# 24 key columns for the edge units of a neighbourhood attention, stacked products for the meta tokens, and the merges' weights split in an earlier stage

## The chip, the cores and the metric

The kernel runs on one core of a Trainium2 chip. The metric is the device time of one execution in microseconds (us); lower is better. Times are given as the median of repeated executions. Beside them stands one profiled execution, from which all durations are read.

## What is computed

The reference is one encoder layer, in float32, over two sequences: a prompt of 1024 tokens and a sample of 2048 tokens, each with 16 learned meta tokens in front. Width is 1024. What matters here:

```
xn   = rmsnorm(h) ; proj = xn @ w_in + b_in          # 1024 -> 6672 columns
ya   = neighbourhood_attention(q, k, v, rpb) * silu(z) @ w_a
yb   = bidirectional_mlstm(...) * silu(z) @ w_b
y    = (sigmoid(ga) * ya + sigmoid(gb) * yb) @ w_out
out  = h + rmsnorm(y)                                # meta rows are dropped
```

The attention has 8 heads of 64. Tokens lie on a grid 64 wide. A query at column c sees 8 rows of keys and the 16 key columns from c0 = clip(c-8, 0, 48), plus the 16 meta tokens. Sixteen neighbouring query columns form a column block (four per grid row), and the reference takes 32 key columns for each block. For the first block (c from 0 to 15) c0 is 0 to 7, so its windows need key columns 0 to 22; for the last block c0 is 40 to 48, so they need columns 40 to 63. The two middle blocks need 31 columns each.

## The kernel before

**Precision.** Every float32 product is made of three products in a rounded format (`fp32r`): a value x is split into a high part xh (rounded by ScalarE with a copy) and a low part xl (x minus xh, by VectorE). Then `xh*wh + xh*wl + xl*wh` is summed in PSUM. `mm3` (L166 to L171) issues these three.

**Two streams of work, one order.** The program is written as two Python generators. `dense` (L1658) walks through `PLAN` (L41): groups of projection columns for a token range ("m" for the mLSTM's columns, "n" for the attention's, "g" for the merge gates), then six "f" entries, the final merges of 512 tokens each. `sparse` walks through `STEPS` (L42): mLSTM of the prompt, attention of the prompt, mLSTM of the sample (the long mLSTM), attention of the sample. Each generator yields costs in us that the author wrote in by hand; `run` (L1703) lets the dense stream advance until its costs have paid for the last sparse step. An attention unit yields four times `A_NA` = 1.085, so some 4.3 us of dense products lie between two units. The order of TensorE's instructions is the order in which these generators issue them. The order on the other engines and in the DMA queues is chosen by a scheduler that simulates the program.

**Weights.** The weights come in units of 128 partitions by up to 1056 values. `requests` (L661) writes the list of units in the order of use; "i" and "t" are the input projection's, "m" the merge's (w_a over w_b, 8 units) and "o" the output projection's (8 units). `wload` (L233) fetches at most two raw units ahead. `wpump` (L244) turns a unit into its two parts: the first time by a split (ScalarE at L263, VectorE at L264) after which both parts are also written to DRAM (`wflush`, L276), later by two loads of 512 KB each (L256). At most `NBW` = 4 units are out at a time (four buffers each for `whi` and `wlo`); `wtake` hands units to a job and `wdone` gives a buffer back. Before the change the "m" and "o" units are first met in the first final merge, and split there.

**Projection.** `fm_half` (L541) makes 128 output channels for 512 tokens with the weights as the stationary operand; `fm_evac` takes them out of PSUM. `tm_unit` (L570) makes 256 or 264 channels token by token with the tokens as the stationary operand (L590 to L592). In the first two groups it also does the 16 meta tokens: three products for each of 8 contraction steps with a stationary operand of only 16 columns.

**The first group.** The row scales of the prompt are not known when its products start. So `group` (L691) keeps the evacuations of the first columns back (`late`), gives them PSUM banks by a list of tags, and issues the product that spreads the row scales over the partitions (`rrows`, L317) inside a chosen column: column `lu` = 2 in the first half, `lu` = 3 in the second (L721).

**Attention.** A head works through four units, one for each column block (`cb`), over 8 query rows. `na_prep` (L817) loads and splits q, k and v for the next head in six steps spread over the units of the present one. It loads k twice, into partitions 0 to 63 and 64 to 127 (`twice`, L743), and rounds both at once into `kd` (L855); partitions 64 to 127 of the stationary operand hold the low part of q. For a unit `na_scores` (L867) issues two products over `ns` x 32 key columns (L877, L878; ns is 12, 13 or 16 rows, one of which holds the meta tokens), and VectorE adds the bias table (L881). `na_exp` takes the exponential, `na_scale` divides by the sum, `na_turn` transposes the probabilities in four blocks of 8 columns (L908) and rounds them (L910), `na_low` makes the low part (L915), and `na_out` multiplies by v, one product for each block (L923). There are 48 heads and 192 units; half of the units are edge units (`cb` 0 or 3).

**Merge.** `final` (L1496) makes `ya @ w_a` and `yb @ w_b` with `mm3`, gates and adds them, and multiplies by w_out (L1569 to L1571).

Of the kernel before, what the change touches and what calls it, by code (L numbers as in the profile page):

```python
# [17 lines left out]
P = 128  # L18
# [3 lines left out]
NM = 16  # L22
# [20 lines left out]
KC0 = (0, 8, 24, 32)  # L43
OFFC = (15, 7, 7, -1)
# [27 lines left out]
def _consts():  # L72
    onehot = np.zeros((64, 4, 8, 16), np.float32)
    for cb in range(4):
        for ic in range(16):
            c0 = min(max(cb * 16 + ic - 8, 0), 48)
            onehot[c0, cb, :, ic] = 1.0
    for ir in range(8):
        onehot[49 + ir, :, ir, :] = 1.0
    masks = np.zeros((3, 64, 16, 64), np.float32)  # L80
    R = 32
    for typ, tl in ((0, 0), (1, 1), (2, R // 8 - 1)):
        _, lo, n = _row_types(R)[tl]
        slots = list(range(lo, lo + n))
        slots = [None] + slots if typ == 2 else slots + [None]
        for si, row in enumerate(slots):
            for c0 in range(49):
                m = np.full(64, NEG, np.float32)
                if row is None:
                    m[(8 if c0 < 24 else 32):][:NM] = 0.0  # L90
# [30 lines left out]
class K:  # L121
# [122 lines left out]
    def wpump(self, most=NBW, parts=1, copy=None):  # L244


        nc, wp = self.nc, self.wp
        self.wload()
        while self.wraw and self.wout < most:
            key, raw, nk, w = self.wraw.popleft()  # L250
            n = nk * w
            hi = wp.tile([P, 4 * WU], F32R, name="whi", bufs=NBW)
            lo = wp.tile([P, 4 * WU], F32R, name="wlo", bufs=NBW)
            if raw is None:
                for x, d in zip((hi, lo), self.wkept[key]):
                    nc.sync.dma_start(x[:, :n].bitcast(F32), d[:, :])  # L256
            else:
                for a in range(parts):
                    c = slice(a * n // parts, (a + 1) * n // parts)
                    if copy:  # L260
                        copy(hi[:, c], raw[:, c])
                    else:
                        nc.scalar.activation(hi[:, c], raw[:, c], AF.Copy)  # L263
                    nc.vector.tensor_tensor(lo[:, c], raw[:, c], hi[:, c].bitcast(F32), op=ALU.subtract)  # L264
# [16 lines left out]
    def wtake(self, n):  # L281
        self.wpump()
        return [self.wrdy.popleft() for _ in range(n)]
# [69 lines left out]
    def opening(self, xp):  # L353
# [45 lines left out]
        self.wrp = wp, 2  # L399

# [93 lines left out]
    def fm_evac(self, col, s, t0, meta, chunks, ps):  # L494
# [39 lines left out]
        if meta and C_NK <= col < C_NV:  # L534
            km = wp.tile([P, 64], F32, name="km", bufs=1)
            nc.gpsimd.memset(km, 0.0)
            nc.gpsimd.tensor_copy(km[:, 8:24], st[:, :NM])
            nc.gpsimd.tensor_copy(km[:, 32:48], st[:, :NM])
            nc.sync.dma_start(self.NKM[(col % 512) // P][:, :], km)
# [30 lines left out]
    def tm_unit(self, col, halves, wd):  # L570
# [10 lines left out]
        for j, (x, s, c, n, cnt, tok) in enumerate(todo):  # L581
            st = wp.tile([P, 2, WU], F32, name="stT", bufs=4)
            for a in range(cnt):
                p = self.psum("pj", [P, 512])
                o = p[:n, :wd]
                xs = slice(c + a * P, c + a * P + n)
                for k in range(KT):
                    wh, wl = ws[k // 4][0][:, k % 4, :], ws[k // 4][1][:, k % 4, :]
                    xh, xl = x[0][:, k, xs], x[1][:, k, xs]
                    nc.tensor.matmul(o, xh, wh, start=k == 0, stop=False)  # L590
                    nc.tensor.matmul(o, xh, wl, start=False, stop=False)  # L591
                    nc.tensor.matmul(o, xl, wh, start=False, stop=k == KT - 1)  # L592
                    if k == 3:
                        if j == len(todo) - 1 and a == cnt - 1:
                            self.wdone()
                        yield 12 * C256
                if j == len(todo) - 1 and a == cnt - 1:
                    self.wdone()
                if s == 0:
                    r = 8 if tok is None else tok // P + a  # L600
# [5 lines left out]
                yield 12 * C256  # L606

    def tm_store(self, col, wd, s, n, cnt, tok, st):
# [30 lines left out]
        else:  # L639
            if tok is None:  # L640
                for lo in (8, 32):
                    nc.sync.dma_start(self.NVM[lo:lo + NM, f:f + wd], st[:n, 0, :wd])
# [18 lines left out]
    def requests(self):  # L661

        unit = {k: j for j, k in enumerate(_weight_units())}
        for s, t0, cols in PLAN:
            if s == "f":
                keys = [("m", f, P) for f in range(KT)] + [("o", c, a) for c in range(4) for a in range(2)]
# [24 lines left out]
    def group(self, s, t0, meta, cols, reuse, nxt):  # L691
# [4 lines left out]
        for j, (kind, c) in enumerate(jobs):  # L696
# [7 lines left out]
            for hf in range(2):  # L704
# [37 lines left out]

    def twice(self, out, d, r0, c0):  # L743

        for a in (0, 64):
            self.nc.sync.dma_start(out[a:a + 64], d[r0:r0 + 64, c0:c0 + out.shape[1]])
# [70 lines left out]
    def na_prep(self, np_, s, rows, heads, j):  # L817
# [14 lines left out]
        self.twice(kr[:, rs:rs + nr, :].rearrange("p a b -> p (a b)"), self.NK[s][pr], h0, lo * 64)  # L832
        self.twice(kr[:, ms, :], self.NKM[pr], h0, 0)
# [20 lines left out]
        with self.held():  # L854
            nc.scalar.activation(kd[:, :ns, :], kr[:, :ns, :], AF.Copy)  # L855
        yield
        nc.vector.tensor_tensor(kx[0:64, :ns, :], kr[0:64, :ns, :], kd[0:64, :ns, :].bitcast(F32), op=ALU.subtract)
# [9 lines left out]
    def na_scores(self, np_, unit, rows):  # L867
# [8 lines left out]
        so = sc[:, :N].rearrange("p (a b) -> p a b", b=32)  # L876
        nc.tensor.matmul(so, stk[:, cb, :], kd[:, :ns, kc:kc + 32], start=True, stop=False)  # L877
        nc.tensor.matmul(so, qb[:, cb, :], self.kx[hh][:, :ns, kc:kc + 32], start=False, stop=True)  # L878
# [3 lines left out]
            out=so, in0=so, in1=gt[:, g0:g0 + ns, c0:c0 + 32],  # L882
            op0=ALU.add, op1=ALU.min, scale=-1.0, scalar=3.0e38, accum_out=mx)
        unit[3] = (pr_, mx, N)
        unit[6] = sc

    def na_exp(self, np_, unit):
        nc = self.nc
        (pr_, mx, N), sc = unit[3], unit[6]
        sm = np_.tile([P, 1], F32, name="sm", bufs=4)  # L890
        nc.scalar.activation(pr_[:, :N].rearrange("p (b a c) -> p b a c", b=4, c=8),
                             sc[:, :N].rearrange("p (a b c) -> p b a c", b=4, c=8),
                             AF.Exp, bias=mx, scale=-1.0, accum_out=sm)
        unit[3] = (pr_, sm, N)

    def na_scale(self, np_, unit):
        nc = self.nc
        pr_, sm, N = unit[3]
# [3 lines left out]
    def na_turn(self, np_, unit):  # L902
        nc = self.nc
        pr_, _, N = unit[3]
        ks = N // 4
        pt = self.psum("tr", [P, 4, P])
        for ch in range(4):
            nc.tensor.transpose(pt[:ks, ch, :], pr_[:, ch * ks:(ch + 1) * ks], self.ident)  # L908
        pts = np_.tile([P, 4, 2, P], F32R, name="pts", bufs=2)
        nc.scalar.activation(pts[:ks, :, 0, :], pt[:ks], AF.Copy)  # L910
        unit[4], unit[6] = pts, pt

    def na_low(self, unit):
        pts, pt, ks = unit[4], unit[6], unit[3][2] // 4
        self.nc.vector.tensor_tensor(pts[:ks, :, 1, :], pt[:ks], pts[:ks, :, 0, :].bitcast(F32), op=ALU.subtract)  # L915

    def na_out(self, unit):
        nc = self.nc
        vt, cb, (_, _, N), pts = unit[0][3], unit[2], unit[3], unit[4]
        ks, kc = N // 4, KC0[cb]  # L920
        av = self.psum("sm", [P, 512])
        for ch in range(4):
            nc.tensor.matmul(av[:, :256], vt[:ks, kc // 8 + ch].rearrange("p a b -> p (a b)"),  # L923
                             pts[:ks, ch].rearrange("p a b -> p (a b)"), start=ch == 0, stop=ch == 3)
# [733 lines left out]
    def dense(self, ctx):  # L1658
# [3 lines left out]
        self.requests()  # L1662
        self.xp = ExitStack()
# [5 lines left out]
        for j, (s, t0, cols) in enumerate(PLAN):  # L1669
# [12 lines left out]
            if not self.done:  # L1682
                z = self.wp.tile([P, 64], F32, name="km", bufs=1)
                self.nc.gpsimd.memset(z, 0.0)
                for lo in (0, 24, 48, 56):
# [3 lines left out]
    def sparse(self):  # L1689

        for kind, s, rts in STEPS:
# [4 lines left out]
            else:  # L1696
                types = _row_types(SEQLEN[s] // 64)
# [81 lines left out]
```

## Time and profile before

| what | value |
|---|---|
| median of 3 executions | 2786.84 us (2786.1 to 2787.6) |
| the profiled execution's own time | 2792.15 us |
| its span, first to last instruction | 2790.4 us |
| mean granted TensorE clock | 0.997 |
| TensorE products | 17120 records |
| DMA | 655.09 MB, mean 235 GB/s |

Stages in the profiled execution, in us from the span's start: mLSTM of the prompt within 298 to 760, attention of the prompt 760 to 1130, long mLSTM 1176 to 1927, attention of the sample 1927 to about 2676. The final merges start at about 2091 and run to the end, the first one to 2215.

A "timeline" row gives the start, the duration, the engine, the source line, the operation, the tile written and the tiles read, and the shape. The duration of a product contains its way through the array, and products overlap; what one costs in a stream is the distance from its start to the next start. A "waits" row gives the total, the number and the longest of the waits of one line for another. A "windows" row gives, for a stretch, each engine's busy time with its instruction count, then the granted clock, the DMA share and GB/s. A "groups" row ends in: busy us, mean ns of one | idle time before them, and what ended it.

### The profile page before, as it was taken

Reading aid. Unit: us, or ns where it says so; the run is one execution under the profiler, and the core shown is the slowest. Engines: PE = TensorE matmul, PEld = TensorE weight load, DVE = VectorE, ACT = ScalarE, POOL = GpSimd, SP = SyncE. Lnnn points to the kernel's source line nnn. Section 1 sums busy time; section 2 is a strip of 40 time slices with the busy share of each in tenths; the row PEclk is TensorE's granted clock in tenths of the full one; section 3 lists DMA queues with packets and bytes.
Section 4 is the critical chain, followed back from the end, with each engine's and each line's share of the span. In section 5 each row is a group of like instructions: output and inputs, shape, how many; then the busy total and the mean of one; then the engine's idle time right before and its main releaser. Section 6 shows DMA issues by size and latency. Waiting matters only on the chain.

```text
span 2790.4 us, 48772 instructions
## 1 busy us (share of the span) xinstructions
PE 2764.9 (99%) x17120; PEld 2461.8 (88%) x17120; DVE 1828.0 (66%) x5075; ACT 1311.8 (47%) x3183; POOL 16.3 (1%) x103
## 2 busy tenths in 40 slices
PE   9999999999999999999999999999999999999998
PEld 7998898999899988988988888888888988889898
DVE  5232688676556655457767666584679888797954
ACT  5112556445443444255456555463455645445421
POOL 0000000000000000000000000000000000000000
PEclk9999999999999999999999999999999999999999
DMA  9555768755965544685666786666579898988965
GB/s 370 181 186 195 255 199 320 269 179 184 338 216 179 173 151 147 187 300 173 205 199 210 254 290 192 190 197 185 179 228 352 278 324 258 316 276 281 329 236 210
DMA packets 378277, 655.09 MB, mean 235 GB/s; under 512 B 50896, under 2 KB 199840, under 8 KB 378032
## 3 DMA queue, kind: packets, MB, share of 16 engines
q1 hardware_dynamic: 376912, 649.29, 70.5%
q0 software_dynamic: 1120, 2.69, 0.4%
q8 instruction: 135, 2.21, 0.3%
q14 instruction: 110, 0.90, 0.1%
HBM read 449.61 MB, written 202.22 MB: 234 GB/s over the span
## 4 chain that ended last, share of the span: by engine, by line
PE 92%; DMA 5%; DVE 2%; ACT 1%; issue 0%; SPq 0%; DVEq 0%; ACTq 0%
PE pj L169 16%; PE pj L170 16%; PE pj L171 16%; PE pj L590 7%; PE pj L591 7%; PE pj L592 7%; PE sm L923 3%; PE pj L1569 3%; PE pj L1571 3%; PE pj L1570 3%; PE tr L908 3%; DMA wraw<-wu 1%; DMA whi<-wh 1%; PE sm L171 1%; PE sm L170 1%; PE sm L169 1%
## 5 line engine op out<-in xcount | busy, mean ns | idle before, releaser
L169 PE MATMUL pj<-xh,whi 128*128 128x512 f32 (+1 forms) x1792 | 705.4, 394 | 1.5 <-ACT whi L263 1.3
L170 PE MATMUL pj<-xl,whi 128*128 128x512 f32 (+1 forms) x1792 | 689.7, 385 | 0.3 <-DVE xl L335 0.3
L171 PE MATMUL pj<-xh,wlo 128*128 128x512 f32 (+1 forms) x1792 | 688.2, 384 | 0.0
L590 PE MATMUL pj<-whi,xh 128*128 128x256 f32 (+3 forms) x1576 | 449.2, 285 | 1.5 <-ACT st L520 1.5
L591 PE MATMUL pj<-wlo,xh 128*128 128x256 f32 (+3 forms) x1576 | 443.7, 282 | 0.8 <-DMA wlo<-wl 0.8
L592 PE MATMUL pj<-whi,xl 128*128 128x256 f32 (+3 forms) x1576 | 443.6, 282 | 0.0
L171 PEld LDWEIGHTS pj<-xh,wlo 128*128 128x128 f32 x1792 | 337.2, 188 | 71.5 <-DVE wlo L264 0.2
L169 PEld LDWEIGHTS pj<-xh,whi 128*128 128x128 f32 x1792 | 337.3, 188 | 61.8 <-ACT whi L263 2.1
L170 PEld LDWEIGHTS pj<-xl,whi 128*128 128x128 f32 x1792 | 337.7, 188 | 57.5 <-issue 1.0
L590 PEld LDWEIGHTS pj<-whi,xh 128*128 128x128 f32 (+1 forms) x1576 | 293.5, 186 | 3.2 <-ACT st L520 1.9
L591 PEld LDWEIGHTS pj<-wlo,xh 128*128 128x128 f32 (+1 forms) x1576 | 293.1, 186 | 2.1 <-DMA wlo<-wl 1.1
L592 PEld LDWEIGHTS pj<-whi,xl 128*128 128x128 f32 (+1 forms) x1576 | 293.1, 186 | 0.9
L1569 PE MATMUL pj<-whi,mh 128*128 128x256 f32 x768 | 221.6, 289 | 3.6 <-DMA whi<-wh 3.6
L1570 PE MATMUL pj<-wlo,mh 128*128 128x256 f32 x768 | 217.6, 283 | 1.2 <-DMA wlo<-wl 1.2
L1571 PE MATMUL pj<-whi,mlo 128*128 128x256 f32 x768 | 217.7, 283 | 0.0
L915 DVE TENSOR_TENSOR pts<-tr,pts 96x512 fp32r<-96x512 f32 (+2 forms) x192 | 131.8, 686 | 96.0 <-ACT pts L910 95.1
L910 ACT ACTIVATE pts<-tr 96x512 fp32r<-96x512 f32 (+2 forms) x192 | 113.9, 593 | 136.8 <-PE tr L908 136.5
L169 PE MATMUL pj<-yh,whi 128*128 128x512 f32 x384 | 154.4, 402 | 0.0
L1569 PEld LDWEIGHTS pj<-whi,mh 128*128 128x128 f32 x768 | 146.4, 191 | 6.2 <-DMA whi<-wh 4.7
L171 PE MATMUL pj<-yh,wlo 128*128 128x512 f32 x384 | 151.4, 394 | 0.0
L170 PE MATMUL pj<-yl,whi 128*128 128x512 f32 x384 | 150.9, 393 | 0.0
L1570 PEld LDWEIGHTS pj<-wlo,mh 128*128 128x128 f32 x768 | 146.7, 191 | 3.0 <-DMA wlo<-wl 1.4
(283 smaller groups left out, 4990.4 us busy)
## 6 DMA issues: line engine op xcount, KB each, us to landing
whi<-wh SPq DMA_DIRECT2D x176, 512.0 KB
wlo<-wl SPq DMA_DIRECT2D x176, 512.0 KB
wraw<-wu SPq DMA_DIRECT2D x64, 512.0 KB
wh<-whi SPq DMA_DIRECT2D x64, 512.0 KB
wl<-wlo SPq DMA_DIRECT2D x64, 512.0 KB
gt<-st SPq DMA_DIRECT2D x96, 256.0 KB
tg<-gt SPq DMA_DIRECT2D x96, 256.0 KB
xt<-xt SPq DMA_DIRECT2D x32, 512.0 KB
```

What stands on the lines that cost most here:

```text
L169: mm(out, ah, bh, start=start, stop=False)
L170: mm(out, ah, bl, start=False, stop=False)
L171: mm(out, al, bh, start=False, stop=stop)
L590: nc.tensor.matmul(o, xh, wh, start=k == 0, stop=False)
L591: nc.tensor.matmul(o, xh, wl, start=False, stop=False)
L592: nc.tensor.matmul(o, xl, wh, start=False, stop=k == KT - 1)
L908: nc.tensor.transpose(pt[:ks, ch, :], pr_[:, ch * ks:(ch + 1) * ks], self.ident)
L910: nc.scalar.activation(pts[:ks, :, 0, :], pt[:ks], AF.Copy)
L915: self.nc.vector.tensor_tensor(pts[:ks, :, 1, :], pt[:ks], pts[:ks, :, 0, :].bitcast(F32), op=ALU.subtract)
L1569: nc.tensor.matmul(o, mh[:, k, xs], wh, start=k == 0, stop=False)
L1570: nc.tensor.matmul(o, mh[:, k, xs], wl, start=False, stop=False)
L1571: nc.tensor.matmul(o, ml[:, k, xs], wh, start=False, stop=k == KT - 1)
```

## The change

Five edits lie in one diff.

1. Edge units take 24 key columns: column block 3 starts at key column 40, not 32, and blocks 0 and 3 use three blocks of 8 columns, not four. Scores, bias, exponential, scaling, transposes and the products with v shrink with it. The meta tokens' second copy lies at columns 40 to 55.
2. The meta tokens' high and low parts are put side by side in one stationary operand `xmp` of 48 columns (high at 0, zeros, low at 32), so two products do what three did; ScalarE and VectorE add the two halves when they take them out.
3. k is loaded into partitions 0 to 63 alone; a second ScalarE copy makes `kd` for partitions 64 to 127 from the first.
4. In the first group's second half the row-scale product is issued at the end of the third column instead of in the fourth, the first three columns are taken out before the fourth is made, and the fourth gets a `tr` bank.
5. The 16 "m" and "o" units are put into the list of weights one by one, ahead of the jobs of groups 4 to 7 of `PLAN`. Such a unit is split and written to DRAM, takes a place among the four while it waits, and is given back without use when the next job takes its weights. The first final merge then loads the split parts.

```diff
-KC0 = (0, 8, 24, 32)
-OFFC = (15, 7, 7, -1)
+KC0 = (0, 8, 24, 40)
+NKB = (3, 4, 4, 3)
+OFFC = (15, 7, 7, 7)
...
 def wpump
+                if key[0] in "mo":
+                    self.wrdy.append(None)
+                    self.wout += 1
+                    self.wload()
+                    continue
 def wtake
+        while self.wrdy[0] is None:
+            self.wrdy.popleft()
+            self.wdone()
...
 def opening
+        nc.gpsimd.memset(self.xmp[:, :, NM:2 * NM].bitcast(F32), 0.0)
+        for a in range(2):
+            nc.vector.tensor_copy(self.xmp[:, :, 2 * NM * a:2 * NM * a + NM], x[a][:, :, :NM].bitcast(F32))
...
 def tm_unit
+                    if tok is None:
+                        both = self.xmp[:, k]
+                        nc.tensor.matmul(o, both, wh, start=k == 0, stop=False)
+                        nc.tensor.matmul(o, both, wl, start=False, stop=k == KT - 1)
+                    else:
...
+                if tok is None:
+                    nc.scalar.activation(st[:n, 1, :wd], p[2 * NM:2 * NM + n, :wd], AF.Copy)
+                    nc.vector.tensor_tensor(st[:n, 1, :wd], p[:n, :wd], st[:n, 1, :wd], op=ALU.add)
...
 def requests
+        ahead = deque([("m", f, P) for f in range(KT)] + [("o", c, a) for c in range(4) for a in range(2)])
+                    if 4 <= j < 8 and ahead:
+                        keys.append(ahead.popleft())
...
 def group
-                    lu = 3 if hf else 2
-                        if late is not None and u == lu and q == 2:
+                        if late is not None and u == 2 and q == 2 + hf:
                             self.rwait[todo[hf][:2]]()
-                    if late is not None and u == lu:
+                    if late is not None and u == 2:
                         for evac in late:
                             evac()
-                        late = tags = None
+                        late = None
+                        tags = iter(("tr",)) if hf else None
...
 def na_prep
-        self.twice(kr[:, rs:rs + nr, :].rearrange("p a b -> p (a b)"), self.NK[s][pr], h0, lo * 64)
-        self.twice(kr[:, ms, :], self.NKM[pr], h0, 0)
+        nc.sync.dma_start(kr[0:64, rs:rs + nr, :].rearrange("p a b -> p (a b)"), self.NK[s][pr][h0:h0 + 64, lo * 64:(lo + nr) * 64])
+        nc.sync.dma_start(kr[0:64, ms, :], self.NKM[pr][h0:h0 + 64, :])
-            nc.scalar.activation(kd[:, :ns, :], kr[:, :ns, :], AF.Copy)
+            nc.scalar.activation(kd[0:64, :ns, :], kr[0:64, :ns, :], AF.Copy)
+        nc.scalar.activation(kd[64:128, :ns, :], kd[0:64, :ns, :].bitcast(F32), AF.Copy)
...
 def na_scores
-        N, kc, g0 = ns * 32, KC0[cb], (5, 1, 0)[typ]
+        kc, nb, g0 = KC0[cb], NKB[cb], (5, 1, 0)[typ]
+        w, N = 8 * nb, 8 * nb * ns
-        nc.tensor.matmul(so, stk[:, cb, :], kd[:, :ns, kc:kc + 32], start=True, stop=False)
-        nc.tensor.matmul(so, qb[:, cb, :], self.kx[hh][:, :ns, kc:kc + 32], start=False, stop=True)
+        nc.tensor.matmul(so, stk[:, cb, :], kd[:, :ns, kc:kc + w], start=True, stop=False)
+        nc.tensor.matmul(so, qb[:, cb, :], self.kx[hh][:, :ns, kc:kc + w], start=False, stop=True)
 def na_turn
-        for ch in range(4):
+        for ch in range(nb):
             nc.tensor.transpose(pt[:ks, ch, :], pr_[:, ch * ks:(ch + 1) * ks], self.ident)
 def na_out
-        for ch in range(4):
+        for ch in range(nb):
```

The masks and the zero rows of the meta tokens' v move with edit 1, and the `xmp` tile has a pool of its own that is closed before the first attention.

More of the change, by code (lines that the diff above doesn't have):

```diff
@@ L588, in tm_unit @@
                     wh, wl = ws[k // 4][0][:, k % 4, :], ws[k // 4][1][:, k % 4, :]
[L589 to L592, printed above, removed]
+                    if tok is None:
[3 more added lines that the diff above has]
+                    else:
+                        xh, xl = x[0][:, k, xs], x[1][:, k, xs]
+                        nc.tensor.matmul(o, xh, wh, start=k == 0, stop=False)
+                        nc.tensor.matmul(o, xh, wl, start=False, stop=False)
+                        nc.tensor.matmul(o, xl, wh, start=False, stop=k == KT - 1)
                     if k == 3:
@@ L640, in tm_store @@
             if tok is None:
-                for lo in (8, 32):
+                for lo in (8, 40):
                     nc.sync.dma_start(self.NVM[lo:lo + NM, f:f + wd], st[:n, 0, :wd])
@@ L663, in requests @@
         unit = {k: j for j, k in enumerate(_weight_units())}
-        for s, t0, cols in PLAN:
+        ahead = deque([("m", f, P) for f in range(KT)] + [("o", c, a) for c in range(4) for a in range(2)])
+        for j, (s, t0, cols) in enumerate(PLAN):
             if s == "f":
+                assert not ahead
                 keys = [("m", f, P) for f in range(KT)] + [("o", c, a) for c in range(4) for a in range(2)]
@@ L881, in na_scores @@
         nc.vector.tensor_tensor_reduce(
-            out=so, in0=so, in1=gt[:, g0:g0 + ns, c0:c0 + 32],
+            out=so, in0=so, in1=gt[:, g0:g0 + ns, c0:c0 + w],
             op0=ALU.add, op1=ALU.min, scale=-1.0, scalar=3.0e38, accum_out=mx)
-        unit[3] = (pr_, mx, N)
+        unit[3] = (pr_, mx, nb, 8 * ns)
         unit[6] = sc
@@ L888, in na_exp @@
         nc = self.nc
-        (pr_, mx, N), sc = unit[3], unit[6]
+        (pr_, mx, nb, ks), sc = unit[3], unit[6]
+        N = nb * ks
         sm = np_.tile([P, 1], F32, name="sm", bufs=4)
-        nc.scalar.activation(pr_[:, :N].rearrange("p (b a c) -> p b a c", b=4, c=8),
-                             sc[:, :N].rearrange("p (a b c) -> p b a c", b=4, c=8),
+        nc.scalar.activation(pr_[:, :N].rearrange("p (b a c) -> p b a c", b=nb, c=8),
+                             sc[:, :N].rearrange("p (a b c) -> p b a c", b=nb, c=8),
                              AF.Exp, bias=mx, scale=-1.0, accum_out=sm)
-        unit[3] = (pr_, sm, N)
+        unit[3] = (pr_, sm, nb, ks)
     def na_scale(self, np_, unit):
         nc = self.nc
-        pr_, sm, N = unit[3]
+        pr_, sm, nb, ks = unit[3]
+        N = nb * ks
         nc.vector.reciprocal(sm, sm)
@@ L903, in na_turn @@
         nc = self.nc
[L904 to L905 removed]
+        pr_, _, nb, ks = unit[3]
         pt = self.psum("tr", [P, 4, P])
[L907 removed]
+        for ch in range(nb):
             nc.tensor.transpose(pt[:ks, ch, :], pr_[:, ch * ks:(ch + 1) * ks], self.ident)
         pts = np_.tile([P, 4, 2, P], F32R, name="pts", bufs=2)
[L910 removed]
+        nc.scalar.activation(pts[:ks, :nb, 0, :], pt[:ks, :nb], AF.Copy)
         unit[4], unit[6] = pts, pt
     def na_low(self, unit):
[L914 to L915 removed]
+        pts, pt, (_, _, nb, ks) = unit[4], unit[6], unit[3]
+        self.nc.vector.tensor_tensor(pts[:ks, :nb, 1, :], pt[:ks, :nb], pts[:ks, :nb, 0, :].bitcast(F32), op=ALU.subtract)
     def na_out(self, unit):
         nc = self.nc
[L919 to L920 removed]
+        vt, cb, (_, _, nb, ks), pts = unit[0][3], unit[2], unit[3], unit[4]
+        kc = KC0[cb]
         av = self.psum("sm", [P, 512])
[L922 removed]
+        for ch in range(nb):
             nc.tensor.matmul(av[:, :256], vt[:ks, kc // 8 + ch].rearrange("p a b -> p (a b)"),
[L924 removed]
+                             pts[:ks, ch].rearrange("p a b -> p (a b)"), start=ch == 0, stop=ch == nb - 1)
         unit[6] = av
@@ L1662, in dense @@
         self.requests()
+        self.mpool = ExitStack()
+        mpool = self.mpool.enter_context(tc.tile_pool(name="mm", bufs=1, side="right", reuse_waits="tile"))
+        self.xmp = mpool.tile([P, KT, 48], F32R, name="xmp")
         self.xp = ExitStack()
@@ L1684, in dense @@
                 self.nc.gpsimd.memset(z, 0.0)
-                for lo in (0, 24, 48, 56):
+                for lo in (0, 24, 32, 56):
                     self.nc.sync.dma_start(self.NVM[lo:lo + 8, :].rearrange("a (b c) -> (a b) c", c=64), z[0:64])
@@ L1696, in sparse @@
             else:
+                self.mpool.close()
                 types = _row_types(SEQLEN[s] // 64)
```

20 lines of the change are left out of this document (9 added, 11 removed).

## The prediction

> **What bounds the kernel now.** I read the page first, then the chain, then who TensorE waits for.
>
> ```profile
> PE 2764.9 (99%) x17120; PEld 2461.8 (88%) x17120; DVE 1828.0 (66%) x5075; ACT 1311.8 (47%) x3183; POOL 16.3 (1%) x103
> ...
> PE 92%; DMA 5%; DVE 2%; ACT 1%; issue 0%; SPq 0%; DVEq 0%; ACTq 0%
> ```
>
> TensorE is busy 99% of the span, and 92% of the chain that ended last lies on it. Busy time alone would not prove the point, since products overlap. The waits of TensorE do:
>
> ```profile
> PE pj L1569 <- DMA whi<-wh: 3.6, 3, 2.7
> ...
> PE pj L590 <- ACT st L520: 1.5, 1, 1.5
> PE pj L169 <- ACT whi L263: 1.3, 1, 1.3
> PE pj L1570 <- DMA wlo<-wl: 1.2, 1, 1.2
> ```
>
> The largest sum over 2790 us is 3.6 us, and no single wait is longer than 2.7 us. So a TensorE instruction that disappears shortens the kernel by its distance to the next start, wherever it stands; work on VectorE, ScalarE and in the queues counts only if it makes a new wait. By stage, the covers differ (columns: stretch, length, busy time of PE, PEld, DVE, ACT, POOL with counts, clock, DMA share, GB/s):
>
> ```profile
> 1176.00:1927.00 751.00, 751.00 (x3923) 635.48 (x3922) 502.47 (x1643) 407.20 (x1073) 4.09 (x22) 1.00 0.68 220
> ...
> 2091.00:2215.00 124.00, 121.85 (x792) 110.47 (x791) 108.93 (x233) 74.31 (x166) 0.51 (x1) 0.98 0.93 321
> 2215.00:2337.00 122.00, 120.02 (x788) 108.27 (x787) 103.01 (x243) 62.16 (x155) 0.00 (x0) 1.00 0.95 293
> ```
>
> Beside the long mLSTM (first row) VectorE is busy 502 of 751 us and DMA 0.68. In the merges (the first two are shown) VectorE is busy 88% and 84%, and DMA 0.93 and 0.95. That is the stage where a gain on TensorE could turn into a wait.
>
> **Edit 1, edge units.** Half of 192 units are edge units, so 96 each lose a transpose and a product with v, and get narrower scores. Two units of the timeline give the prices:
>
> ```profile
> 2201.09 0.40 PE L877 MATMUL sc<-kd,stk 128*128 128x512 f32 x1
> 2201.32 0.40 PE L878 MATMUL sc<-kx,qB 128*128 128x512 f32 x1
> 2201.55 0.28 PE L1569 MATMUL pj<-whi,mh 128*128 128x256 f32 x1
> ...
> 2202.99 0.60 PE L908 MATMUL tr<-ident,prb 128*128 128x128 f32 x4
> 2203.35 0.36 PE L1569 MATMUL pj<-whi,mh 128*128 128x256 f32 x1
> ...
> 2204.86 0.63 PE L923 MATMUL sm<-pts,vt 128*128 128x256 f32 x4
> 2205.33 0.28 PE L1569 MATMUL pj<-whi,mh 128*128 128x256 f32 x1
> ```
>
> Four transposes take 2203.35 - 2202.99 = 0.36 us, 0.09 each; four products with v 0.47, 0.1175 each. So 96 x 0.09 = 8.6 us and 96 x 0.1175 = 11.3 us go. A score product of 512 columns costs 0.23. The other widths:
>
> ```profile
> 1020.53 0.35 PE L877 MATMUL sm<-kd,stk 128*128 128x416 f32 x1
> 1020.73 0.35 PE L878 MATMUL sm<-kx,qB 128*128 128x416 f32 x1
> ...
> 803.06 0.34 PE L877 MATMUL sc<-kd,stk 128*128 128x384 f32 x1
> 803.24 0.34 PE L878 MATMUL sc<-kx,qB 128*128 128x384 f32 x1
> 803.41 0.28 PE L590 MATMUL pj<-whi,xh 128*128 128x264 f32 x1
> 803.53 0.29 PE L591 MATMUL pj<-wlo,xh 128*128 128x264 f32 x1
> ```
>
> 416 columns cost 0.20, 384 cost 0.175 and 264 cost 0.12. The new widths are 384 (from 512), 312 (from 416) and 288 (from 384), a third of the units each. No row shows 312 or 288. They lie between 264 and 384, so between 0.12 and 0.175; the line through both gives 0.142 and 0.131. Savings are 0.055, 0.058 and 0.044 per product, 0.052 on the mean, and 2 x 96 x 0.052 = 10.0 us. Edit 1 takes 29.9 us. VectorE and ScalarE lose work in the same units:
>
> ```profile
> L881 DVE CUSTOM_DVE_ANT_1 sc<-sc,gt 128x512 f32<-128x512 f32 x32 | 22.2, 692 | 5.2 <-PE sc L878 4.8
> ...
> L881 DVE CUSTOM_DVE_ANT_1 sc<-sc,gt 128x384 f32<-128x384 f32 x32 | 18.1, 565 | 21.3 <-PE sc L878 15.7 <-DMA gt<-rpb 4.3 <-issue 0.6
> ```
>
> L881 falls by 692 - 565 = 127 ns for a quarter less; the low parts at L915 shrink by the same 128 elements and the scaling by less, so a unit gets some 0.3 us of VectorE back, about what TensorE gets. I count this at nothing, since TensorE doesn't wait for it.
>
> **Edit 2, meta products.** Five token units have meta tokens, 8 steps each: 40 products go of 120, two of every three stay. One unit's 24, first to last, and the row behind them:
>
> ```profile
> 94.78 0.28 PE L590 MATMUL pj<-whi,xh 128*16 128x264 f32 x1
> ...
> 97.68 0.28 PE L590 MATMUL pj<-whi,xh 128*128 128x264 f32 x1
> ```
>
> They take 2.90 us, 0.121 each, so 40 x 0.121 = 4.8 us. The stationary operand grows from 16 to 48 columns; the neighbours with 128 columns cost the same 0.12, so the width is free. Five short adds on two engines, and the memset and two copies at the start, are hidden: the start waits for the first weights (17.83 to 25.19 in the chain):
>
> ```profile
> 17.83 7.36 DMA wraw<-wu
> ```
>
> If the cover were gone, two copies would cost under 1 us.
>
> **Edit 3, one load of k and a second copy.** TensorE sees only the lead of `kd` before the head's first score:
>
> ```profile
> 863.60 0.83 ACT L855 ACTIVATE kd<-kr 128x768 fp32r<-128x768 f32 x1
> ...
> 870.33 0.35 PE L877 MATMUL sc<-kd,stk 128*128 128x384 f32 x1
> ```
>
> It ends at 864.43, 5.9 us before its use. The second copy is as long as the first, 0.83 us here and up to 1.06 for 1024 columns:
>
> ```profile
> L855 ACT ACTIVATE kd<-kr 128x1024 fp32r<-128x1024 f32 x16 | 16.9, 1056 | 1.3 <-DMA kr<-nkm 1.3
> ```
>
> Queued on ScalarE behind it are the rounding of v and the exponentials; each is late by at most 1 us. I take zero; all of it exposed would be rival C. SP issues 96 fewer loads, and half of k's bytes go.
>
> **Edit 4, the second half of the first group.** The wait for L520 above is this one:
>
> ```profile
> 57.51 0.40 PE L171 MATMUL tr<-xh,wlo 128*128 128x512 f32 x1
> 59.42 0.39 PE L590 MATMUL pj<-whi,xh 128*128 128x264 f32 x1 [1.51 <-ACT st L520]
> ```
>
> The token unit needs a `pj` bank and all three are let go only after the fourth column. After the change they are let go a column earlier. A column is 24 products of 512 columns at 0.23 us, 5.5 us, more than the wait. The row-scale product now stands behind 18 of the fourth column's 24 products and will stand ahead of them. That column ends near 57.7, so it began near 51 (its 5.5 us and under 1 us for the row-scale product). The scales' last piece ends near 47.4, as ScalarE's row shows:
>
> ```profile
> 46.71 0.68 ACT L312 ACTIVATE xr<-ident,nwy 128x128 f32<-128x128 f32 x2
> ```
>
> So 1.5 us go. Bounds: 0 to 1.9 us.
>
> **Edit 5, the merges' units ahead.** Sixteen splits leave the first merge and go beside earlier stages, the long mLSTM above all:
>
> ```profile
> L264 DVE TENSOR_TENSOR wlo<-wraw,whi 128x1024 fp32r<-128x1024 f32 x61 | 74.5, 1221 | 25.3 <-ACT whi L263 24.5 <-PE sm L1358 0.6
> ...
> L263 ACT ACTIVATE whi<-wraw 128x1024 fp32r<-128x1024 f32 x61 | 64.6, 1059 | 105.5 <-PE pj L170 51.4 <-PE pj L592 46.1 <-DMA wraw<-wu 4.6
> ```
>
> That is 16 x 1.22 = 19.5 us of VectorE and 16 x 1.06 = 17 us of ScalarE, put into a stage with 249 and 344 us idle. DMA there gets 16 raw reads and 32 writes of 0.5 MB, 25 MB beside 220 GB/s x 751 us = 165 MB: the share goes from 0.68 to about 0.78. In the first merge the two waits of this window are those that splits in the two queues can explain:
>
> ```profile
> PE sm L923 <- ACT prb L891: 2.1, 1, 2.1
> PE sm L877 <- DVE yg L938: 2.0, 1, 2.0
> ```
>
> They are worth 4.1 us. In their place the first merge loads both parts, as later merges do; those wait for weights 3.6 + 1.2 = 4.8 us over the four that run beside attention, 1.2 each. Net gain 2.9 us. Bounds: a loss of 16 x 2.7 = 43 us if every unit waits as long as the longest above, a gain of 4.1. I take the merge's own neighbours. In the list of weights the extra place costs a job one column of lead, and the load behind an ahead unit can go into its buffer as soon as its two writes have landed, so no lead is lost where a token unit follows a token unit. Cover: a column is 5.6 us of products, and a load takes:
>
> ```profile
> 774.35 6.37 DMA wlo<-wl
> ```
>
> **Sum.** 29.9 + 4.8 + 1.5 + 2.9 = 39.1 us from a span of 2790.4, 1.4%. The profiled execution took 2792.15, the median is 2786.84; off the median the result is 2747.7, rounded to **2748 us**.
>
> **Weighed against the Trainium skill.** The widths' prices rest on weight loads that don't set the pace. Their row:
>
> ```profile
> L171 PEld LDWEIGHTS pj<-xh,wlo 128*128 128x128 f32 x1792 | 337.2, 188 | 71.5 <-DVE wlo L264 0.2
> ```
>
> "TensorE: Matmul & The Clock Gate", section "LDWEIGHTS (loading the stationary operand)", in the Trainium skill says that a weight load overlaps a running product only where they use different row groups. By that rule a new width under the load's time would save nothing (rival B); the trace disagrees, with 264 columns and a fresh load every 0.12 us.
>
> **The rivals.** A: the merges are really held by DMA (0.93 to 0.95) and VectorE (84 to 88%), and TensorE only looks full; then edge units beside them save nothing. The sample's attention runs from 1927 to 2676 and the merges start at 2091, so 585 of its 749 us, 50 of its 64 edge units, lie beside them: 50 x (0.104 + 0.09 + 0.1175) = 15.6 us, and the 2.9 of edit 5, are lost: 2766. Against it: the waits there are few, and both covers shrink with the same units. B: a pair of load and product can't go below 0.188 us; narrower scores save nothing below the 384 row's 0.175, only 0.23 to 0.188 and 0.20 to 0.188, for 64 x 0.042 + 64 x 0.012 = 3.5 us: 2754. Against it: 17120 x 0.188 = 3219 us, more than the span. C: the second copy of k lies on the path of every head: 48 heads of 0.83 to 1.06 us, mean 0.93, give 44.6 us: 2792, about as before. It needs the lead of 5.9 us to vanish. D, the other side: a split of an ahead unit waits at the head of ScalarE's in-order queue for its buffer, evacuations behind it are late, and TensorE runs out of banks. The L263 row shows the hold, 105.5 us before 61 splits, 1.7 each. At 1.7 + 1.06 + 1.22 = 4.0 us for each of 16, 64 us: 2748 + 64 = 2812. It decides from 39.1 / 16 = 2.4 us a unit. Against it: before, 52 other splits held ScalarE the same way and TensorE waited for L263 once, 1.3 us. That edit 5 doesn't do what it says (other work made the two waits) costs 2.9: 2751, inside the forecast.
>
> **How the numbers follow.** Forecast 0.72, own range 2738 (all weight waits gone too) to 2756; A 0.15; B 0.04; C 0.04; D 0.05. A measurement tells 0.2%, 5.6 us, from no change: faster means below 2781.3. Faster 0.72 + 0.15 + 0.04 = 0.91; C counts as same, 0.04; D as slower, 0.05. For 8 in 10 the range takes the forecast's and A's: 2738 to 2768.
>
> **What would show it.** Edge units with three transposes and three products; score products of 288 and 312 columns near 0.13 and 0.14 us; 80 meta products; no wait at the first token unit; no L263 between 2050 and 2200, and sixteen more near 1000 to 1700. Wrong would be: new waits of TensorE in the merges (A), distances of 0.19 us at 288 columns (B), L877 waiting for `kd` (C), or waits for evacuations around the moved splits (D).

## The result, and the profile after

The changed kernel takes 2754.14 us (2751.11 to 2755.42), the kernel before 2786.47 us in the same comparison: ratio 0.9883, 95% interval 0.9866 to 0.9900, so 28 to 37 us less. Two later comparisons of the same two kernels gave 0.9874 (0.9860 to 0.9889) and 0.9871 (0.9857 to 0.9884). The forecast was 2748 with a range of 2738 to 2768. The time lies in the range, 6 us above the forecast. The gain that the forecast gave, 39.1 us, is 2 to 7 us more than the three comparisons; it lies above the interval of the first and at the upper edge of the other two (31 to 39 and 32 to 40), so how much is missing is itself known to a few us only.

The two profiled executions show a larger difference, 2792.15 to 2751.11 = 41.0 us. They are two single executions: the first lay 5.7 us above its median, the second 3.0 us below. What is read from them below is where time went, not how much in all.

The page of the kernel after, the lines that answer to those of before:

```profile
PE 2726.5 (99%) x16888; PEld 2430.0 (88%) x16888; DVE 1801.9 (66%) x5082; ACT 1341.2 (49%) x3236; POOL 16.1 (1%) x104
...
PE 92%; DMA 5%; DVE 2%; ACT 1%; issue 0%; SPq 0%; DVEq 0%; ACTq 0%
```

TensorE has 232 products fewer (2 x 96 of edit 1 and 40 of edit 2) and is as full as before, 99%. The bound is the same. The edge units are as forecast. The timeline of the kernel after shows three transposes, three products with v, and the two new widths:

```profile
2193.05 0.49 PE L931 MATMUL tr<-ident,prb 128*128 128x128 f32 x3
2193.30 0.48 PE L170 MATMUL pj<-yh,whi 128*128 128x512 f32 x1
...
2194.77 0.52 PE L946 MATMUL sm<-pts,vt 128*128 128x256 f32 x3
2195.12 0.33 PE L899 MATMUL sm<-kd,stk 128*128 128x384 f32 x1
```

```profile
802.60 0.30 PE L899 MATMUL sc<-kd,stk 128*128 128x288 f32 x1
802.74 0.29 PE L900 MATMUL sc<-kx,qB 128*128 128x288 f32 x1
802.87 0.29 PE L607 MATMUL pj<-whi,xh 128*128 128x264 f32 x1
```

```profile
1020.30 0.30 PE L899 MATMUL sc<-kd,stk 128*128 128x312 f32 x1
1020.44 0.30 PE L900 MATMUL sc<-kx,qB 128*128 128x312 f32 x1
1020.58 0.40 PE L170 MATMUL pj<-xh,whi 128*128 128x512 f32 x1
```

Up to the next start, three transposes take 0.25 us where four took 0.36, so the one that went was worth 0.11; three products with v take 0.35 for 0.47. A product of 288 columns costs 0.135 us and one of 312 costs 0.14; the line through 264 and 384 had given 0.131 and 0.142.

TensorE's waits in the kernel after, the seven largest sums:

```profile
PE pj L608 <- DMA wlo<-wl: 2.6, 2, 1.7
PE pj L1593 <- DMA wlo<-wl: 1.7, 3, 1.0
PE sm L946 <- ACT prb L914: 1.5, 3, 0.7
PE sm L1006 <- issue: 1.5, 1, 1.5
PE pj L607 <- DMA whi<-wh: 1.4, 1, 1.4
PE sc L899 <- ACT kd L877: 1.1, 1, 1.1
PE pj L1592 <- DMA whi<-wh: 1.0, 1, 1.0
```

The wait of the first token unit (L590 for L520, 1.5 us before) is gone, as edit 4 was to do. So are most of the two waits of the first merge. Waits for weights in the merges (now L1592 and L1593) fell from 4.8 to 2.7; in the profiles of the two later comparisons the same kernel has 4.1 and 3.5, so such a sum moves by 1.4 us from one execution to the next. Three kinds are new or larger: the second copy of k at one head (L899, 1.1), weights of token units (L607 and L608, 4.0 where L591 had 0.8, as the prompt's attention opens), and the gates of the long mLSTM (L1006, 1.5).

The long mLSTM and the first two merges, by stretches of the kernel after (columns as before):

```profile
1176.00:1927.00 751.00, 749.96 (x3898) 633.50 (x3897) 509.91 (x1651) 417.60 (x1083) 4.11 (x22) 1.00 0.72 243
2074.80:2190.30 115.50, 115.50 (x768) 105.52 (x767) 92.74 (x222) 66.53 (x161) 0.51 (x1) 1.00 0.83 271
2190.30:2306.20 115.90, 115.57 (x765) 105.36 (x764) 98.76 (x243) 66.22 (x158) 0.00 (x0) 1.00 0.91 297
```

The first merge, 124 us before, takes 115.5 and TensorE is busy in all of them; VectorE is down from 88% to 80% and DMA from 0.93 to 0.83. No split (now L264) starts after 1682 us, where the last one of the kernel before started near 2188.

### The profile page after: what moved, and what is told of

Its sections match the earlier page's. It is cut to its first block, busy times and chain, and to the rows that moved or that the text cites. A ratio compares the mean times of both kernels' runs of the same rounds, so it can differ in the third digit from the quotient of the medians.

```text
span 2749.3 us, 48199 instructions
## 1 busy us (share of the span) xinstructions
PE 2726.5 (99%) x16888; PEld 2430.0 (88%) x16888; DVE 1801.9 (66%) x5082; ACT 1341.2 (49%) x3236; POOL 16.1 (1%) x104
## 4 chain that ended last, share of the span: by engine, by line
PE 92%; DMA 5%; DVE 2%; ACT 1%; issue 0%; SPq 0%; DVEq 0%; ACTq 0%
PE pj L170 17%; PE pj L171 16%; PE pj L172 16%; PE pj L607 6%; PE pj L608 6%; PE pj L609 6%; PE pj L1593 3%; PE pj L1594 3%; PE pj L1592 3%; PE sm L946 3%; PE tr L931 2%; DMA wlo<-wl 1%; PE sm L172 1%; DMA wraw<-wu 1%; PE sm L171 1%; PE sm L170 1%
## 5 line engine op out<-in xcount | busy, mean ns | idle before, releaser
L607 PE MATMUL pj<-whi,xh 128*128 128x256 f32 (+1 forms) x1536 | 439.6, 286 | 1.4 <-DMA whi<-wh 1.4
L608 PE MATMUL pj<-wlo,xh 128*128 128x256 f32 (+1 forms) x1536 | 433.2, 282 | 2.6 <-DMA wlo<-wl 2.6
L609 PE MATMUL pj<-whi,xl 128*128 128x256 f32 (+1 forms) x1536 | 433.0, 282 | 0.0
L608 PEld LDWEIGHTS pj<-wlo,xh 128*128 128x128 f32 x1536 | 289.9, 189 | 3.3 <-DMA wlo<-wl 3.1
L607 PEld LDWEIGHTS pj<-whi,xh 128*128 128x128 f32 x1536 | 290.0, 189 | 2.2 <-DMA whi<-wh 1.7
L609 PEld LDWEIGHTS pj<-whi,xl 128*128 128x128 f32 x1536 | 289.9, 189 | 0.0
L1593 PE MATMUL pj<-wlo,mh 128*128 128x256 f32 x768 | 216.8, 282 | 1.7 <-DMA wlo<-wl 1.7
L1592 PE MATMUL pj<-whi,mh 128*128 128x256 f32 x768 | 217.3, 283 | 1.0 <-DMA whi<-wh 1.0
L938 DVE TENSOR_TENSOR pts<-tr,pts 96x384 fp32r<-96x384 f32 (+2 forms) x192 | 119.1, 620 | 75.9 <-ACT pts L933 73.9
L933 ACT ACTIVATE pts<-tr 96x384 fp32r<-96x384 f32 (+2 forms) x192 | 103.8, 541 | 123.3 <-PE tr L931 122.5
L1593 PEld LDWEIGHTS pj<-wlo,mh 128*128 128x128 f32 x768 | 145.5, 189 | 3.6 <-DMA wlo<-wl 2.5
L1592 PEld LDWEIGHTS pj<-whi,mh 128*128 128x128 f32 x768 | 145.6, 190 | 2.3 <-DMA whi<-wh 1.2
```

What stands on the lines that cost most here:

```text
L933: nc.scalar.activation(pts[:ks, :nb, 0, :], pt[:ks, :nb], AF.Copy)
L938: self.nc.vector.tensor_tensor(pts[:ks, :nb, 1, :], pt[:ks, :nb], pts[:ks, :nb, 0, :].bitcast(F32), op=ALU.subtract)
L1592: nc.tensor.matmul(o, mh[:, k, xs], wh, start=k == 0, stop=False)
L1593: nc.tensor.matmul(o, mh[:, k, xs], wl, start=False, stop=False)
```

## The experiments

Each run was timed beside the kernel before on the same chip. The question was how 39.1 us forecast became 32 to 37: which term was wrong.

**Edit 1 alone.** The diff is the attention's part of the change, on the kernel before.

> The kernel before with edit 1 alone (24 key columns in edge units). The prediction's own term: 29.9 us less, so about 2756.5. All five edits together gave 32.3 less where 39.1 was forecast. If the shortfall of 7 us is in this term (products cheaper to drop than counted, or part of the relief lost beside the merges), it shows here: 22 to 25 us less. If the shortfall is in edit 3 or edit 5, this run keeps its 28 to 32.

Measured: 2761.49 us, ratio 0.9903 (0.9890 to 0.9917), 27.0 us less with an interval of 23 to 31. The forecast's 29.9 lies in it. TensorE's waits in the merges stayed:

```profile
PE pj L1572 <- DMA whi<-wh: 5.7, 2, 5.5
PE sm L879 <- DVE yg L941: 2.5, 2, 2.1
PE pj L1573 <- DMA wlo<-wl: 1.0, 1, 1.0
```

In this execution they sum to 6.7 us, where the kernel before had 4.8, so narrower units alone don't relieve the weight loads. The time also answers rival A: with nothing saved beside the merges the term would have been 29.9 - 15.6 = 14.3 us, outside the interval.

**Edits 2 and 4 alone.**

> The kernel before with edits 2 and 4 (two meta products for three; the row scales a column earlier). The prediction's terms: 4.8 + 1.5 = 6.3 us less, about 2780. If the shortfall sat here: 0 to 3 less.

Measured: 2784.23 us, 0.9986 (0.9975 to 0.9998), 3.9 us less, interval 0.6 to 7. The forecast's 6.3 lies in it; the value itself is smaller. Two waits of its profile bear on what follows. As the prompt's attention opens, TensorE waits 1.8 us for `kd`, though this kernel has no second copy. And the waits of the first merge, 4.1 us before, are 1.2 here, though nothing was changed near it.

**Edit 3 alone.**

> The kernel before with edit 3 alone (k loaded once, second copy on ScalarE). The prediction: 0. A rival: the wait for kd of 1.1 us and the waits around 750 to 776 that stand in the profile after come from the second copy at the first heads; then 3 to 6 us more. If the copy lay on every head: 44 more.

Measured: 2780.53 us, 0.9977 (0.9968 to 0.9986): 6.4 us less, interval 4 to 9. Neither the forecast's zero nor the rival's loss. TensorE's waits from 2050 to 2660 in this run are these two and no others:

```profile
PE sm L919 <- ACT prb L887: 2.3, 2, 1.6
PE sm L873 <- DVE yg L934: 1.9, 1, 1.9
```

The two waits of the first merge are there as before. The waits for weights, 4.8 us before, are not, and the one of a token unit (L591, 0.8) is gone too.

**Edit 3 with its loads put back.** The suspected cause alone is undone:

```diff
+        nc.sync.dma_start(kr[64:128, rs:rs + nr, :].rearrange("p a b -> p (a b)"), self.NK[s][pr][h0:h0 + 64, lo * 64:(lo + nr) * 64])
+        nc.sync.dma_start(kr[64:128, ms, :], self.NKM[pr][h0:h0 + 64, :])
```

> The kernel before with edit 3, but k is loaded into partitions 64 to 127 as well; nothing reads that half, ScalarE still makes the second copy. If edit 3's 6.4 us come from the 96 loads and the bytes that went (shorter waits for weights in the merges), they are gone: 0 within 2 us of the kernel before, and waits for weights in the merges of 3 to 6 us. If they come from the other order of ScalarE's and VectorE's work: 4 to 8 us less stay.

Measured: 2788.78 us, 1.0004 (0.9996 to 1.0013): the gain is gone. Waits from 2050 to 2660:

```profile
PE sm L921 <- ACT prb L889: 4.1, 3, 1.8
PE pj L1567 <- DMA whi<-wh: 3.3, 2, 2.9
PE sm L875 <- DVE yg L936: 1.9, 1, 1.9
```

The wait for weights in the merges is back, 3.3 us, and so are those of the token units, 1.1 us between 745 and 800. The page's DMA lines of the two runs, first edit 3 alone, then with the loads back:

```profile
DMA packets 370597, 644.33 MB, mean 232 GB/s; under 512 B 46288, under 2 KB 195232, under 8 KB 370352
```

```profile
DMA packets 378278, 655.10 MB, mean 235 GB/s; under 512 B 50896, under 2 KB 199840, under 8 KB 378032
```

So 10.8 MB of 655, and 96 loads, are worth 6 us in a kernel where TensorE waits for other loads of the same queue. The DMA share over the first four merges (2091 to 2580) is 0.85 to 0.92 without these loads and 0.91 to 0.97 with them. The waits for weights in the merges, 3.3 to 4.8 us, are between half and three quarters of the 6.4 us; where the rest went was not worked out. The bytes, the number of loads and the other order of the queue were not taken apart.

**Edit 5 alone.**

> The kernel before with edit 5 alone (merge weights split ahead). The prediction: 2.9 us less. A rival: the waits near 1137 and 1183 in the profile after, where an ahead split stands in the queues just as the long mLSTM opens, come from it, and the first merge gains 4 and loses it again: 0 to 3 us more.

Measured: 2788.60 us, 0.9995 (0.9987 to 1.0004), between 3.6 us less and 1.1 more. The two waits of the first merge fell from 4.1 to 0.8 us, and it has no wait for weights. Others came: the second and the third merge wait 1.5 and 4.9 us for weights, and there are two waits around the opening of the long mLSTM (L169 for `kth` and L995):

```profile
PE pj L1581 <- DMA whi<-wh: 4.9, 1, 4.9
...
PE sm L169 <- ACT kth L1211: 1.8, 1, 1.8
PE sm L935 <- ACT prb L903: 1.5, 2, 0.8
...
PE pj L1582 <- DMA wlo<-wl: 1.5, 1, 1.5
...
PE sm L995 <- PE pj L600: 1.0, 1, 1.0
```

Behind the wait on `kth` (L1211) stands a load. ScalarE's timeline of the same run, in brackets its idle time before the instruction and what ended it:

```profile
1194.96 0.51 ACT L1094 ACTIVATE cv<-raw,cw 128x256 f32<-128x256 f32 x1 [4.64 <-DMA raw<-mk]
1195.37 0.36 ACT L1211 ACTIVATE kth<-tr 128x256 fp32r<-128x256 f32 x1
```

ScalarE stood idle 4.64 us until the mLSTM's load `raw<-mk` landed, and the rounding of `kth` was queued behind the instruction that needed the load. What in edit 5 made this load late was not followed further.

**All five, all but edit 3, all but edit 5, and edit 5 one group later** (`if 5 <= j < 9 and ahead` in `requests`).

> All five edits again, beside the kernel before on the chip that the other runs of this call use. If the four parts add up (ratios 0.9903, 0.9986, 0.9977, 0.9995 multiply to 0.986), it comes out 38.7 us below the kernel before. If the parts disturb each other, some 32 us below, as in the first comparison.

> All but edit 3: k is loaded twice again. If edit 3 alone is worth 6.4 us, as its own run says, through shorter weight loads in the merges, this is 6 us slower than all five, and TensorE's waits for weights in the merges come back (3 to 6 us). If it is worth nothing beside the others: the same as all five.

> All but edit 5: the merges' weights are split in the first merge again. By the prediction 2.9 us slower than all five. By its own run (1.4 less, unclear), the same within 3 us. If moving the splits is what the other parts suffer from (the waits at 1137 and 1183 and those at 753 to 776), it is 3 to 6 us faster than all five.

> All five, with the merges' units ahead of the jobs of groups 5 to 8, one group later. If the splits at 1112 and 1142 and the loads between them cause the waits at 1137 and 1183, those 3 us go and the first merge keeps its gain: 2 to 4 us faster than all five. If the waits belong to the opening of the long mLSTM: no change.

| kernel | us | ratio to before | interval |
|---|---|---|---|
| all five | 2752.67 | 0.9874 | 0.9860 to 0.9889 |
| all but edit 3 | 2759.90 | 0.9893 | 0.9876 to 0.9910 |
| all but edit 5 | 2749.64 | 0.9862 | 0.9847 to 0.9876 |
| edit 5 one group later | 2750.30 | 0.9861 | 0.9846 to 0.9876 |

Without edit 3 it is 7.2 us slower, and the waits for weights in the merges come back: 4.3 + 2.6 us in that run's profile, against 2.7, 4.1 and 3.5 in the three profiles of all five. Without edit 5 it is 3.0 us faster, and with edit 5 one group later 2.4 us faster. The intervals of the last two rows overlap that of all five, so neither difference is shown by this comparison alone.

**Products back, and all but edit 5 again.** One run gives work back to TensorE alone, one repeats the kernel without edit 5, and one is their control, all five:

```diff
             nc.tensor.transpose(pt[:ks, ch, :], pr_[:, ch * ks:(ch + 1) * ks], self.ident)
+        if nb < 4:
+            nc.tensor.transpose(pt[:ks, 3, :], pr_[:, 2 * ks:3 * ks], self.ident)
...
+        if nb < 4:
+            nc.tensor.matmul(av[:, 256:512], vt[:ks, kc // 8 + 2].rearrange("p a b -> p (a b)"),
+                             pts[:ks, 2].rearrange("p a b -> p (a b)"), start=True, stop=True)
```

> All five edits, but each edge unit makes its fourth transpose and its fourth product with v again, from the third block and into PSUM that nobody reads. TensorE alone gets work back. If TensorE sets the time everywhere, 96 x (0.09 + 0.1175) = 19.9 us more than all five by the prediction's prices, up to 21.7 if a transpose counts 0.108. If the merges are held by DMA and VectorE (rival A), 4 to 6 us more, the prompt's part alone.

> All five edits as the control of this call: 32 to 36 us below the kernel before.

> All but edit 5 beside its control. If edit 5 costs in company what the last call showed: 2 to 4 us faster than the control. If that was chance: within 1.5 us of it, or slower by the 2.9 of the prediction.

Control 2752.33 us; products back 2773.29; all but edit 5 2749.87 (0.9862, 0.9847 to 0.9878). The 192 instructions cost 2773.29 - 2752.33 = 21.0 us, 0.218 for a transpose and a product. The forecast's prices gave 19.9. By the scatter of the nine executions the 21.0 are good to some 4 us. Without edit 5 it is again faster, by 2.5 us. Over both comparisons, eight executions each, the kernels with and without edit 5 are 2.7 us apart, with a 95% interval of about 1 to 5 by their scatter: edit 5 costs in company.

The run with the products back shows what a transpose costs. Its fourth one is L933:

```profile
2204.28 0.49 PE L931 MATMUL tr<-ident,prb 128*128 128x128 f32 x3
2204.60 0.27 PE L933 MATMUL tr<-ident,prb 128*128 128x128 f32 x1
2204.63 0.48 PE L170 MATMUL pj<-yh,whi 128*128 128x512 f32 x1
2204.95 0.39 PE L171 MATMUL pj<-yl,whi 128*128 128x512 f32 x1
```

Three transposes take 0.32 us up to the fourth, 0.11 each. The product behind the fourth starts 0.03 us after it and then takes 0.32 us to the next start, where such a product takes 0.23 elsewhere.

**Where edit 5 loses.** At the opening of the long mLSTM the gates' load stands in SP's queue. The queue in the kernel after:

```profile
1123.32 0.32 SPq L964 DMA_DIRECT2D ya<-yg  x1
1124.96 3.41 SPq L669 DMA_DIRECT2D nv<-stT  x3
...
1130.31 0.55 SPq L979 DMA_DIRECT2D g_t<-gg  x1
```

and in the last run, without edit 5:

```profile
1122.64 0.32 SPq L952 DMA_DIRECT2D ya<-yg  x1
1124.28 0.58 SPq L661 DMA_DIRECT2D nv<-stT  x1
...
1126.80 0.55 SPq L967 DMA_DIRECT2D g_t<-gg  x1
```

The two lines left out load two constants, the same in both. Behind `ya`, three stores of v, which wait for VectorE, stand ahead of the gates' load instead of one. After `ya` the load goes out 7.0 us later instead of 4.2. VectorE's first gate step waits for it, and TensorE's first gate product (L1006) stands behind VectorE's steps; the profile gives no releaser for its wait ("issue"):

```profile
1134.13 0.35 DVE L989 TENSOR_SCALAR g_lf<-g_t 128x68 f32<-128x68 f32 x2 [0.70 <-DMA g_t<-gg]
...
1138.27 0.30 DVE L1000 TENSOR_TENSOR g_lf<-g_lf,g_e 128x136 f32<-128x136 f32 x1
1138.67 0.63 PE L1006 MATMUL sm<-g_lf,tri 128*128 128x68 f32 x4 [1.45 <-issue]
```

In the run without edit 5, TensorE's waits between 960 and 1210 sum to 0.2:

```profile
PE sm L1062 <- DVE g_wT L1058: 0.2, 1, 0.2
```

With edit 5 one group later, the same 0.2 us are the only wait there, and the time is 2.4 us under all five.

The other runs agree with this reading. In the profiles of all five, and of all but edit 3, the load goes out 7.0 us after `ya` and the first gate product waits 1.3 to 1.5 us; with edit 5 alone it is 7.9 us and 1.0 us (L995 there). In the kernel before, and with the products back, it goes out 5.0 to 5.1 us after `ya`, behind two stores, and there is no wait. The kernel with the products back has edit 5, so the edit doesn't bring the late load in every order of the queue. And the wait of 1.5 us is about half of the 2.7 that edit 5 costs; the rest was not found.

## Why the prediction was right, and where it was not

**The bound** was right. 21.0 us for the 192 instructions given back, against 19.9 by the start-to-start distances, shows that TensorE sets the time and that these distances are the prices, to within the 4 us of that run. Rival A falls with it (4 to 6 us), and with the 27.0 us of edit 1 alone, where A gives 14.3. Rival B falls with the 0.135 us at 288 columns, and the 0.175 us at 384 already lay under its 0.188; that the time came out at B's 2754 us is chance.

**Edit 1**: right within its interval, 27.0 (23 to 31) for 29.9. The transpose was undersized, 0.11 for 0.09: the mean over four divides a group whose last member overlaps the next instruction. With 0.11 the term is 31.8, just above the interval, so a few us of what TensorE was spared did not arrive. The waits for weights in the merges, 6.7 us for 4.8, are a candidate from one execution; the cause stays open.

**Edits 2 and 4**: 3.9 (0.6 to 7) for 6.3, not told apart from it. The wait of 1.5 us went, and 0.9 us more of waits stand at the opening of the prompt's attention (2.3 for 1.4).

**Edit 3** is the step that failed. It was put at zero because `kd` had 5.9 us of lead, and of its loads the text only said that they fall away. That lead was read at a later head, and it held everywhere but at the first: TensorE waits for `kd` at one head, 1.1 us in the kernel after, and rival C falls. Even that wait is not the second copy's alone, since edits 2 and 4 without it have 1.8 us and all but edit 3 has 0.8. But the loads that go were worth 6.4 us alone and 7.2 in company, for the larger part in the waits for weights of the merges. The rows were at hand: those waits, 4.8 us, and DMA shares of 0.93 and 0.95 beside them. A forecast that called DMA the danger of that stage should have counted a saving there.

**Edit 5** failed in sign: 2.9 us of gain forecast, nothing to be told from zero alone, a loss of 3.0 and 2.5 us in company. Its first part was right for edit 5 alone: the two waits of the first merge shrink from 4.1 to 0.8 us, and no wait for weights stands there. In company there was little left to gain: without edit 5 the first merge has 1.2 and 1.8 us of waits in the two profiles, with it 0.7. The forecast had counted the whole 4.1 for edit 5, and with the other edits in place most of it was gone already. The other thing missed is the move past a queue. The stage with idle engines has a place where the chain is short of lead, the opening of the mLSTM, and there the order of SP's queue changed. The sentence on the DMA share (0.68 to 0.78; measured 0.72) answered the wrong question. The prediction also set a load of 6.37 us beside a cover of 5.6 and drew no conclusion from the load being the longer. Rival D had the place of the loss and the wrong mechanism: what came late was the gates' load in the kernel after, and the load `raw<-mk` ahead of `kth` with edit 5 alone, not an evacuation. About half of the loss stays unexplained.

**The sum.** The single terms measured add to 27.0 + 3.9 + 6.4 + 1.4 = 38.7 us; together they give 32 to 37. Edit 5's loss in company covers some 4 of the difference. The rest, up to 2 us, stays open. Waits of 4.2 to 5.1 us at the opening of the prompt's attention, 1.4 before, stand in the three profiles of all five edits. Edits 2 and 4 alone, which bring that stage forward, have 2.3 us there, all of it for `kd` and `kx` and none for weights; the two profiles of all but edit 5 have 1.7 and 4.7.

That the total came so near the forecast is in part luck. A gain of 6.4 us that was put at nothing stands against a loss where 2.9 us of gain were forecast and against two terms that came out 2 to 3 us smaller; without edit 3, which was forecast to change nothing, the kernel took 2759.9 us, outside the forecast's own range of 2738 to 2756 and inside the stated one only because that one takes in rival A's times.

All but edit 5 has the lowest medians, 2749.6 and 2749.9 us in two comparisons, 3.0 and 2.5 under the changed kernel beside it; edit 5 one group later, 2750.3, is not told apart from it.

## What to carry to other kernels

When one engine is full, price an edit on it by start-to-start distances, and check by giving the work back; the distance of an edit's last instruction to whatever follows can hide part of its cost. Then price every other edit by the queue it loads or unloads in the stage where that queue is busy: a load taken away beside a DMA share of 0.9 can be worth more than the work it was replaced with costs. Work moved to an idle stage is moved into that stage's queues too; look for the one instruction there that has no lead.

## What the runs showed of the hardware

A stationary operand of 48 columns costs TensorE what one of 16 cost. One unit's 16 products in the kernel after, first to last, and the row behind them:

```profile
92.88 0.28 PE L603 MATMUL pj<-whi,xmp 128*48 128x264 f32 x1
...
94.80 0.29 PE L607 MATMUL pj<-whi,xh 128*128 128x264 f32 x1
```

They take 1.92 us, 0.120 each, where the products with 16 columns took 0.121.

Products of 288 and 312 columns follow each other in 0.135 and 0.14 us, each with a weight load of 0.19 us:

```profile
L899 PEld LDWEIGHTS sc<-kd,stk 128*128 128x128 f32 x96 | 18.2, 190 | 3.4 <-ACT kd L877 1.5
```

The load does not set the pace. The rule of the Trainium skill that the prediction weighed stands in "TensorE: Matmul & The Clock Gate" under "The mechanism": a weight load overlaps running products only where their row groups differ. By it alone these products should have cost the load's time; the measurement decides against it. The same section also lets a load run ahead into a background weight buffer; no run here shows whether that is what happens.
